# Up projection of a trunk kernel on Trainium2: in four of ten pairs, a second group of four feature blocks by seven products

## The chip, the cores and the metric

The kernel runs on one core of a Trainium2 chip. The metric is the device time of one execution in microseconds (us); a run's time is the median over several executions. The engines are named as in the profile: PE is TensorE (PEld its weight loads), DVE is VectorE, ACT is ScalarE, POOL is GpSimd, SP is SyncE, whose queue issues most weight loads.

## The reference, cut to what matters

One layer (DEPTH = 1), 256 tokens, width 2048, all in float32: a mixer, then a gated MLP, whose up projection is the subject.

```python
D_MODEL = 2048; SEQ = 256; DEPTH = 1; D_FF = 5632; CONV_FFN = 3
...
        x = x + jnp.einsum('bsd,de->bse', mixed, w_out[l])

        h = rmsnorm(x, norm_ffn_w[l])
        gate, up = jnp.split(jnp.einsum('bsd,df->bsf', h, w_up[l]), 2, axis=-1)
        gate = causal_dwconv(gate, conv_ffn_w[l]) + conv_ffn_b[l]
        x = x + jnp.einsum('bsf,fd->bsd', jax.nn.gelu(gate, approximate=False) * up, w_down[l])
    return rmsnorm(x, norm_final_w)
```

`w_up` has 2 x 5632 columns: gate and up.

## The kernel before, in words

**Precision by parts.** Every weight tile (256 rows by 512 columns, 512 KB, held as 128 x 1024) is split into a high part (`whi`, a cast on ACT) and a low part (`wlo`, raw minus high on DVE); the activations `fhl` have such parts too. A product is high x high, low x high and high x low: three matmuls of 128 x 512 for each 128 rows. The function `begin` makes the split of the next tile in the list `srcs`; `weights` hands tiles to PE and keeps two more begun. There are three buffers each of `whi` and `wlo` and four of `raw`, loaded by SP.

**Pairs.** The up projection works through 11 pairs c = 0 to 10: 512 gate columns with 512 up columns. The 256 tokens are two halves t. A plain step takes one weight tile `("plain", c, col, kp)` (col 0 gate, 1 up; kp one of eight row tiles of 256) and multiplies it with both token halves: 12 matmuls.

**Seven products.** From pair 1 on, the first four feature blocks of 128 (row tiles kp = 0 and 1, `FOUR = 0`) are done otherwise. Their four weight tiles (2 row tiles x gate and up, called quads: b11, b12, b21, b22) and the matching blocks of the activations form a 2 x 2 block product, done in seven products instead of eight: 11, T1, T2, 21, T3, 22, T4, of one weight tile and 6 matmuls each. The products named T take sums of quads, made in place on DVE by `up_sum` (line 195); sums of the activations (`ups`) are made once, by `up_sums`. The partial results meet in PSUM banks through two additions on DVE (lines 1345 and 1357) and copies on ACT.

**Order.** The list `up_steps` is written out by hand, and PE follows it. A pair's gate tiles come first, the last gate tiles alternate with the first up tiles, and the last three up tiles (`TAIL`) are set between the next pair's products T1, 11 and T2. Then follow 21, the transposes of the finished gate (`"gate"`), T3, 22, the transposes of up and T4. The elementwise work on the finished pair (convolution on ACT and DVE, line 1283, then GELU, product with up and a split, `hhi` and `hlo`) is spread over the plain steps after T4. The quads of the next pair are asked for by SP at the steps 8 to 5 ahead of its products, the sum for T1 is called 3 steps ahead. DVE, ACT and SP follow an order that a scheduler derives from the program; only PE's is fixed. Ahead of the up projection stands the output projection, in which the residual is added (`xt`), normed by feature and turned into `fhl`.

Of the kernel before, what the change touches and what calls it, by code (L numbers as in the profile page):

```python
# [8 lines left out]
F32 = mybir.dt.float32  # L9
# [5 lines left out]
P = 128  # L15
S = 256
# [19 lines left out]
def kernel(  # L36
# [58 lines left out]
    NUP = DFF // 512  # L95
    FOUR = 0
    UP_PARTS = ("T1", "11", "T2", "21", "T3", "22", "T4")
# [3 lines left out]
    for c in range(NUP):  # L101
        kps = [kp for kp in range(KD // 2) if c == 0 or kp // 2 != FOUR]
        gate_steps, up_only = ([("plain", c, col, kp) for kp in kps] for col in range(2))
        up_steps += gate_steps[:TAIL]
        for a, b in zip(gate_steps[TAIL:], up_only):
            up_steps += [a, b]
        rest = up_only[-TAIL:]
        if c + 1 == NUP:
            up_steps += rest
            break  # L110
        t1, p11, t2, p21, t3, p22, t4 = [("part", c + 1, what) for what in UP_PARTS]
        up_steps += [("loads", c + 1)]
        up_steps += [t1, rest[0], p11, rest[1], t2, rest[2], p21, ("gate", c), t3, p22, ("up", c), t4]
    for step in up_steps:
        if step[0] == "plain":
            srcs.append(up_w[step[1]][step[2]][step[3]])
        elif step[0] == "part":
            srcs.append(("up", step[1], step[2]))
    down = [cols(w_down[0], 512 * c, KF) for c in range(4)]
# [63 lines left out]
    UP_BUFFER = {"11": 0, "T1": 1, "T2": 1, "T3": 0, "21": 2, "22": 3, "T4": 1}  # L183

    def quad_load(c, n):

        i = (1, 0, 3, 2)[n]
        up_quarters[i] = fp.tile([P, 2, 512], F32, tag=f"xt{i}", name=nm("quad"))
        last_load[0] = nc.sync.dma_start(up_quarters[i], up_w[c][i % 2][2 * FOUR + i // 2]).ins

    def up_sum(what):
        b11, b12, b21, b22 = (up_quarters[i] for i in range(4))
        for out_, plus_, minus_ in {"T1": [(b12, b12, b11)], "T2": [(b12, b22, b12)],
                                    "T3": [(b11, b12, b11), (b12, b21, b12)]}[what]:
            nc.vector.tensor_tensor(out_, plus_, minus_, op=ALU.subtract)  # L195
# [14 lines left out]

    def quarter(half, chunk, what):

        if half == "up":
            return up_quarters[UP_BUFFER[what]]
# [27 lines left out]
    def begin(n):  # L242
        while len(made) < min(len(srcs), n):
            load(len(made) + 1)
            raw = loads[len(made)]
            if isinstance(raw, tuple):
                raw, plus, minus = raw
                nc.vector.tensor_tensor(raw, plus, minus, op=ALU.subtract)
            src = srcs[len(made)]
            following = {"T1": "T2", "T2": "T3"}.get(src[2]) if isinstance(src, tuple) and src[0] == "up" else None  # L250
# [4 lines left out]
            nc.scalar.copy(hi, raw)  # L255
            if shape[1] == 8:
                lo = None
                nc.vector.tensor_tensor(hi[:, :, 32:64], raw[:, :, 0:32], hi[:, :, 0:32].bitcast(F32),
                                        op=ALU.subtract)
            else:  # L260
                lo = wpool.tile(shape, F32R, tag="wlo", name=nm("wlo")) if keep is None else \
                    mtile(4 + keep, shape, F32R, nm("klo"))
                last_split[0] = nc.vector.tensor_tensor(lo, raw, hi.bitcast(F32), op=ALU.subtract).ins  # L263
                splits.append(last_split[0])
            made.append((hi, lo))
            if following is not None:
                up_sum(following)
            if isinstance(src, tuple) and src[0] != "up" and src[2] in ("T1", "T3", "T2", "T4"):
                next_quarter()
# [990 lines left out]

    def up_sums():

        h = fp.tile([P, 4, S], F32, tag="y", name=nm("whole"))
        for j in range(2):
            part = fhl[2 * FOUR + j]
            nc.vector.tensor_tensor(h[:, 2 * j : 2 * j + 2], part[:, :, 0, :].bitcast(F32),
                                    part[:, :, 1, :].bitcast(F32), op=ALU.add)
        b = fp.tile([P, 2, 4, S], F32R, tag="ups", name="ups")
        return four_sums(*by_halves(h), b[:, 0], b[:, 1])

# [20 lines left out]
    def up_part(c, pts):  # L1291
# [8 lines left out]
        else:  # L1300
            hh = fp.tile([P, 4, S], F32R, name=f"hhi{c}")
            hl = fp.tile([P, 4, S], F32R, name=f"hlo{c}")
        nc.scalar.copy(hh, y)
# [24 lines left out]

    def up_product(c, what):

        bank = banks_of.setdefault(c, {})
        if what in ("11", "21", "T4"):
            j, t = {"11": (0, 0), "21": (1, 0), "T4": (1, 1)}[what]
            high, low = (lambda kk, f=f: f(4 * FOUR + 2 * j + kk, t) for f in (fh, fl))
        else:
            n = {"T1": 0, "T2": 1, "T3": 2, "22": 3}[what]
            high, low = (lambda kk, s=s: s[:, n, kk * P : (kk + 1) * P] for s in up_ups[0])
        w = weights()
        if what == "T1":
            bank["own"] = pm()[:, 0]  # L1340
# [5 lines left out]
        ps = {"T1": "own", "21": (0, 0), "22": (1, 0)}.get(what, (0, 1))  # L1346
        high_first([(bank[ps], high, low)], w, what in ("T1", "11"))
        if what == "T1":
            own = cpool.tile([P, 512], F32, tag="sqj", name=nm("own"))
# [44 lines left out]
    for i, step in enumerate(up_steps):  # L1394
        if step[0] == "part":
            up_product(*step[1:])
            if step[2] == "T4":
                def elementwise(c=step[1] - 1, gates=gates, ups=ups):
# [9 lines left out]
        elif step[0] == "plain":  # L1408
            up_plain(*step[1:])
            if step[1:] == (0, 0, 1):  # L1410
                turned_rows()
            if step[1] == 0 and step[2:] == (0, TAIL):
                up_ups.append(up_sums())
            if step[1] == NUP - 1 and step[2] == 0:
# [204 lines left out]
```

## Time and profile before

| | |
|---|---|
| median of three runs | 1553.76 us (1552.94 to 1554.03) |
| the profiled execution, its span | 1553.06 us, 1551.3 us |
| TensorE's mean granted clock | 0.998 |
| busy: PE, PEld, DVE, ACT | 1537.5, 1268.2, 1195.4, 829.8 us |
| output projection, up projection | to about 819 us, 819 to 1307 us |
| one pair of the up projection | about 44.1 us |
| read from HBM | 301.75 MB |

Busy times are sums over the span, in which stages with different limits lie; a stage is read from its own stretch. Times in the views are us from the start of the span. A row of a timeline names its start, its duration, engine, line and operation, then in brackets the idle time ahead of it and what ended that. A load's "us to landing" runs from its issue to its last byte. A row of stretches gives, after the stretch and its length, each engine's busy time and count of instructions, then the granted clock, the mean busy share of the 16 DMA engines and GB/s.

### The profile page before, as it was taken

How to read it: one execution, taken by the hardware profiler on the slowest of the kernel's cores; microseconds unless marked ns; L12 is line 12 of the kernel's file. 1: busy time of each engine (PE TensorE's matmuls, PEld its weight loads, DVE VectorE, ACT ScalarE, POOL GpSimd, SP SyncE). 2: the span in 40 equal slices, each digit the busy share in tenths (PEclk: the TensorE clock that was granted, in tenths of full speed). 3: DMA queues.
4: the chain of work that ended last, by engine and by line, in shares of the span. 5: the costliest groups of instructions: out<-in, count | busy, mean ns of one | idle time of the engine just before them, and what ended most of it. 6: DMA issues, size and time to landing. Idle time of an engine off the chain costs nothing.

```text
span 1551.3 us, 20145 instructions
## 1 busy us (share of the span) xinstructions
PE 1537.5 (99%) x7350; PEld 1268.2 (82%) x7350; DVE 1195.4 (77%) x1713; ACT 829.8 (53%) x1038; POOL 65.1 (4%) x82
## 2 busy tenths in 40 slices
PE   9999999999999999999999999999999999999998
PEld 8888888788878888888887888888888888788886
DVE  6789858996689858887664877778778776878885
ACT  6455446454545445454454666656656665545552
POOL 1010002000100000000000000000000000000100
PEclk9999999999999999999999999999999999999999
DMA  8777757776577656675676666656666667556652
GB/s 273 212 223 211 199 153 226 213 207 182 166 231 211 197 170 200 215 209 181 215 260 205 189 190 182 186 180 199 203 200 190 188 187 267 189 190 204 221 189 92
DMA packets 167697, 310.46 MB, mean 200 GB/s; under 512 B 19458, under 2 KB 23330, under 8 KB 167470
## 3 DMA queue, kind: packets, MB, share of 16 engines
q1 hardware_dynamic: 159456, 287.37, 61.0%
q0 software_dynamic: 4032, 14.68, 2.9%
q10 hardware_dynamic: 4110, 7.13, 1.4%
q8 instruction: 57, 0.93, 0.2%
q14 instruction: 42, 0.34, 0.1%
HBM read 301.75 MB, written 7.38 MB: 199 GB/s over the span
## 4 chain that ended last, share of the span: by engine, by line
PE 96%; DMA 1%; DVE 1%; issue 1%; ACT 0%; POOL 0%; POOLq 0%; DVEq 0%; ACTq 0%
PE psg L1326 29%; PE psm L298 15%; PE psm L300 15%; PE psm L299 15%; PE psm L1311 7%; PE psg L1311 6%; PE psm L444 1%; PE psm L1383 1%; PE psg L343 1%; PE psm L1326 1%; PE psg L834 1%; DVE wlo L263 0%; DMA raw<-in_w_down_dram 0%; PE psg L836 0%; DMA vrow<-ev 0%
## 5 line engine op out<-in xcount | busy, mean ns | idle before, releaser
L255 ACT CAST whi<-raw 128x1024 fp32r<-128x1024 f32 x460 | 484.1, 1053 | 474.5 <-PE psm L299 277.0
L263 DVE TENSOR_TENSOR wlo<-raw,whi 128x1024 fp32r<-128x1024 f32 x458 | 557.1, 1220 | 169.0 <-ACT whi L255 163.2
L263 DVE TENSOR_TENSOR wlo<-quad,whi 128x1024 fp32r<-128x1024 f32 x112 | 137.1, 1224 | 73.2 <-ACT whi L255 71.9
L255 ACT CAST whi<-quad 128x1024 fp32r<-128x1024 f32 x112 | 118.1, 1055 | 107.5 <-PE psg L1326 55.9
L300 PE MATMUL psm<-wlo,xhl 128*128 128x512 f32 x432 | 169.5, 393 | 1.8 <-DVE wlo L263 1.8
L298 PE MATMUL psm<-whi,xhl 128*128 128x512 f32 x432 | 169.0, 391 | 0.0
L299 PE MATMUL psm<-whi,xhl 128*128 128x512 f32 x432 | 168.6, 390 | 0.0
L1326 PE MATMUL psg<-whi,fhl 128*128 128x512 f32 x504 | 127.9, 391 | 0.0
L1326 PEld LDWEIGHTS psg<-whi,fhl 128*128 128x128 f32 x504 | 93.9, 188 | 18.9
L300 PEld LDWEIGHTS psm<-wlo,xhl 128*128 128x128 f32 x432 | 81.1, 188 | 19.2 <-DVE wlo L263 2.6
L298 PEld LDWEIGHTS psm<-whi,xhl 128*128 128x128 f32 x432 | 81.1, 188 | 16.7
L299 PEld LDWEIGHTS psm<-whi,xhl 128*128 128x128 f32 x432 | 81.1, 188 | 16.7
L1326 PE MATMUL psg<-wlo,fhl 128*128 128x512 f32 x252 | 69.9, 389 | 0.0
L1311 PE MATMUL psm<-wlo,hhi 128*128 128x512 f32 (+1 forms) x150 | 58.1, 387 | 0.5 <-DVE wlo L263 0.5
L1311 PE MATMUL psm<-whi,hhi 128*128 128x512 f32 (+1 forms) x150 | 58.2, 388 | 0.2 <-ACT whi L255 0.2
L1311 PE MATMUL psm<-whi,hlo 128*128 128x512 f32 (+1 forms) x150 | 58.0, 386 | 0.0
L1326 PEld LDWEIGHTS psg<-wlo,fhl 128*128 128x128 f32 x252 | 47.3, 188 | 10.0
L195 DVE TENSOR_TENSOR quad<-quad,quad 128x1024 f32<-128x1024 f32 x40 | 49.0, 1225 | 7.5 <-DMA quad<-in_w_up_dram 6.5
L298 PE MATMUL psm<-whi,mhi 128*128 128x512 f32 x128 | 50.9, 397 | 0.0
L1311 PE MATMUL psg<-whi,hhi 128*128 128x512 f32 (+1 forms) x130 | 50.3, 387 | 0.1
L300 PE MATMUL psm<-wlo,mhi 128*128 128x512 f32 x128 | 50.0, 391 | 0.0
L1311 PE MATMUL psg<-whi,hlo 128*128 128x512 f32 (+1 forms) x130 | 50.0, 386 | 0.0
(428 smaller groups left out, 2939.8 us busy)
## 6 DMA issues: line engine op xcount, KB each, us to landing
raw<-in_w_in_dram SPq DMA_DIRECT2D x224, 512.0 KB, 4.3
raw<-in_w_up_dram SPq DMA_DIRECT2D x136, 512.0 KB, 4.6
raw<-in_w_down_dram SPq DMA_DIRECT2D x64, 512.0 KB, 4.7
quad<-in_w_up_dram SPq DMA_DIRECT2D x40, 512.0 KB, 4.5
raw<-in_w_out_dram SPq DMA_DIRECT2D x32, 512.0 KB, 4.0
quad<-in_w_down_dram POOLq DMA_DIRECT2D x24, 512.0 KB, 5.3
mv<-vrow SPq DMA_DIRECT2D x12, 512.0 KB, 4.5
taps<-in_conv_qkv_w_dram SPq DMA_DIRECT2D x16, 256.0 KB, 6.5
```

The costliest lines, as they stand in the source:

```text
L195: nc.vector.tensor_tensor(out_, plus_, minus_, op=ALU.subtract)
L255: nc.scalar.copy(hi, raw)
L263: last_split[0] = nc.vector.tensor_tensor(lo, raw, hi.bitcast(F32), op=ALU.subtract).ins
L298: mm(ps[:, t, :], lh(k, t), hi[:, kk, :], start=(k == 0), stop=False)
L299: mm(ps[:, t, :], ll(k, t), hi[:, kk, :], start=False, stop=False)
L300: mm(ps[:, t, :], lh(k, t), lo[:, kk, :], start=False, stop=(k == nk - 1))
L343: nc.tensor.transpose(pt[:, ff, t * P : (t + 1) * P], src[:, t, f * P : (f + 1) * P], ident)
L444: mm(ps_k0[:, t, :], part(k, t), w[:, kk, :], start=(k == 0 and w is hi and part is xh), stop=(k == KD - 1 and w is lo))
L834: mm(pg0, kq[:, h, 0, 0:P], kq[:, h, :, :], start=True, stop=True)
L1311: mm(ps[:, cs], lhs(kk), part_[:, kk, cs], start=(first and kk == 0 and n == 0), stop=(last and kk == 1 and n == 2), skip_group_check=shared)
L1326: mm(ps, lhs(kk), w[n][:, kk], start=(first and n == 0 and kk == 0 and lhs is high), stop=False, skip_group_check=True)
L1383: nc.tensor.transpose(out_[f // 2][:, f % 2, t * P : (t + 1) * P], e[:, t, f * P : (f + 1) * P], ident)
```

## The change

In pairs 1, 3, 5 and 7 (`TWO`) the feature blocks 4 to 7 (row tiles kp = 2 and 3, group `ch` = 1) are also done by seven products, ahead of group 0 in each place. The seven results of both groups are accumulated in the same banks: group 1 begins them, group 0 ends them. The pair ahead does all its gate tiles first and keeps its last six up tiles (`tail` = 6) for the places between the first six products (T1, 11 of group 1, T1, 11 of group 0, T2 of each). Then come 21, 21, the gate's transposes, T3, T3, 22, 22, up's transposes, T4, T4. The second group's quads live in the buffers of the later `hhi8`, `hlo8`, `hhi9`, `hlo9`, and are asked for in the program 12 to 9 steps ahead of the products, the first group's 6 to 3 steps ahead. The sums of T3 and T4 are now two separate calls, and sums stand behind chosen splits (`sums_behind`).

```diff
-    FOUR = 0
+    TWO = (1, 3, 5, 7)
+    chunks_of = [()] + [(1, 0) if c in TWO else (0,) for c in range(1, NUP)]
...
-        kps = [kp for kp in range(KD // 2) if c == 0 or kp // 2 != FOUR]
+        kps = [kp for kp in range(KD // 2) if kp // 2 not in chunks_of[c]]
...
+        tail = 6 if c + 1 in TWO else TAIL
...
+        parts = [[("part", c + 1, what, ch) for what in UP_PARTS] for ch in chunks_of[c + 1]]
         up_steps += [("loads", c + 1)]
-        up_steps += [t1, rest[0], p11, rest[1], t2, rest[2], p21, ("gate", c), t3, p22, ("up", c), t4]
+        if c + 1 in TWO:
+            first_four = [parts[ch][n] for ch in range(2) for n in (0, 1)] + [parts[ch][2] for ch in range(2)]
+            for a, b in zip(first_four, rest):
+                up_steps += [a, b]
+            p21, t3, p22, t4 = ([parts[ch][n] for ch in range(2)] for n in range(3, 7))
+            up_steps += p21 + [("gate", c)] + t3 + p22 + [("up", c)] + t4
+        else:
+            t1, p11, t2, p21, t3, p22, t4 = parts[0]
+            up_steps += [t1, rest[0], p11, rest[1], t2, rest[2], p21, ("gate", c), t3, p22, ("up", c), t4]
...
+            if src[1] not in TWO:
+                behind = {"T1": [(n, "T2", 0)], "T2": [(n, "T3", 0), (n, "T4", 0)]}.get(what, [])
+            else:
+                behind = {("11", 1): [(n, "T1", 0), (n + 1, "T2", 1)], ("T1", 0): [(n + 1, "T2", 0)],
+                          ("T2", 1): [(n, "T3", 1), (n + 1, "T4", 1)],
+                          ("T2", 0): [(n, "T3", 0), (n + 1, "T4", 0)]}.get((what, ch), [])
...
+    UP_HOMES = (("xt0", "xt1", "xt2", "xt3"), ("hhi8", "hlo8", "hhi9", "hlo9"))
...
-    def up_sums():
+    def up_sums(ch):
...
-    def up_product(c, what):
+    def up_product(c, what, ch):
...
+        begins, ends_ = (ch == chunks_of[c][n] for n in (0, -1))
...
-        for n in range(4):
-            if i + 8 - n < len(up_steps) and up_steps[i + 8 - n][0] == "loads":
-                quad_load(up_steps[i + 8 - n][1], n)
-        if i + 3 < len(up_steps) and up_steps[i + 3][0] == "loads":
-            up_sum("T1")
+        for n, step in enumerate(up_steps):
+            if step[0] == "loads":
+                when = (6, 5, 4, 3, 12, 11, 10, 9) if step[1] in TWO else (8, 7, 6, 5)
+                for q in sorted(range(len(when)), key=lambda q: -when[q]):
+                    if max(n - when[q], 0) == i:
+                        quad_load(step[1], q)
+                if n - 3 == i:
+                    up_sum("T1", chunks_of[step[1]][0])
```

The scheduler places DVE, ACT and SP anew. First, DVE at the beginning of a pair's products; `quad` is a tile of group 0 or 1, `raw` a plain up tile. Before, in pair 2:

```order
L263 TENSOR_TENSOR wlo_1346_7828<-quad_1326_7721,whi_1345_7826 128x1024
L195 TENSOR_TENSOR quad_1326_7721<-quad_1334_7767,quad_1326_7721 128x1024
L263 TENSOR_TENSOR wlo_1350_7850<-raw_1348_7846,whi_1349_7848 128x1024
L263 TENSOR_TENSOR wlo_1352_7866<-quad_1330_7747,whi_1351_7864 128x1024
L195 TENSOR_TENSOR quad_1330_7747<-quad_1326_7721,quad_1330_7747 128x1024
L263 TENSOR_TENSOR wlo_1357_7881<-raw_1355_7877,whi_1356_7879 128x1024
L263 TENSOR_TENSOR wlo_1359_7897<-quad_1326_7721,whi_1358_7895 128x1024
```

and now, in pair 3:

```order
L286 TENSOR_TENSOR wlo_1416_8156<-quad_1383_7991,whi_1415_8154 128x1024
L1331 TENSOR_TENSOR hlo1_8128<-y_1401_8071,hhi1_8127 128x1024
L219 TENSOR_TENSOR quad_1383_7991<-quad_1389_8016,quad_1383_7991 128x1024
L286 TENSOR_TENSOR wlo_1419_8174<-raw_1417_8170,whi_1418_8172 128x1024
L286 TENSOR_TENSOR wlo_1422_8193<-quad_1385_8002,whi_1421_8191 128x1024
L219 TENSOR_TENSOR quad_1385_8002<-quad_1383_7991,quad_1385_8002 128x1024
L286 TENSOR_TENSOR wlo_1426_8207<-raw_1424_8203,whi_1425_8205 128x1024
```

The same alternation of split, sum, split goes on; it now runs over six products in place of three, and the `hlo` of the elementwise work falls between the first split and its sum.

Second, DVE behind the last products. Before, behind pair 2's T4 (its split is the first row):

```order
L263 TENSOR_TENSOR wlo_1375_7980<-quad_1326_7721,whi_1374_7978 128x1024
L1357 TENSOR_TENSOR psg_1376_7988<-psg_1360_7901,own_1354_7875 128x512
L1283 SCALAR_TENSOR_TENSOR y_1387_8041<-psm_1373_7969,cfw_390,y_1387_8041 128x255
L263 TENSOR_TENSOR wlo_1379_7994<-raw_1377_7990,whi_1378_7992 128x1024
L1283 SCALAR_TENSOR_TENSOR y_1387_8041<-psm_1373_7969,cfw_390,y_1387_8041 128x254
L263 TENSOR_TENSOR wlo_1383_8015<-raw_1381_8011,whi_1382_8013 128x1024
L195 TENSOR_TENSOR quad_1391_8073<-quad_1391_8073,quad_1395_8099 128x1024
L1283 SCALAR_TENSOR_TENSOR y_1387_8041<-psm_1373_7969,cfw_390,y_1387_8041 128x255
```

and now behind pair 1's last T3, 22 being split (the splits of the two T4 are the rows from quads):

```order
L1389 TENSOR_TENSOR psg_1329_7710<-psg_1293_7512,own_1299_7548 128x512
L1310 SCALAR_TENSOR_TENSOR y_1347_7789<-psm_1324_7681,cfw_390,y_1347_7789 128x255
L286 TENSOR_TENSOR wlo_1331_7714<-quad_1241_7255,whi_1330_7712 128x1024
L1310 SCALAR_TENSOR_TENSOR y_1347_7789<-psm_1324_7681,cfw_390,y_1347_7789 128x254
L286 TENSOR_TENSOR wlo_1333_7724<-quad_1260_7363,whi_1332_7722 128x1024
L286 TENSOR_TENSOR wlo_1338_7747<-raw_1336_7743,whi_1337_7745 128x1024
L1310 SCALAR_TENSOR_TENSOR y_1347_7789<-psm_1324_7681,cfw_390,y_1347_7789 128x255
L219 TENSOR_TENSOR quad_1383_7991<-quad_1383_7991,quad_1385_8002 128x1024
L286 TENSOR_TENSOR wlo_1342_7761<-raw_1340_7757,whi_1341_7759 128x1024
L1310 SCALAR_TENSOR_TENSOR y_1347_7789<-psm_1324_7681,cfw_390,y_1347_7789 128x254
L286 TENSOR_TENSOR wlo_1346_7775<-raw_1344_7771,whi_1345_7773 128x1024
L219 TENSOR_TENSOR quad_1335_7741<-quad_1335_7741,quad_1339_7755 128x1024
```

The sum in the eighth row now is the T1 sum of pair 3's group 1 (its split stands in the list for pair 3 above), drawn ahead of the split of the second plain gate tile of pair 1; the T1 sum of pair 2 is the last row. It writes into the buffer that pair 1's first T4 was split from.

Third, SP in the output projection. Before:

```order
L179 DMA raw_1168_6847<-in_w_out_dram 128x2x512
L179 DMA raw_1171_6865<-in_w_out_dram 128x2x512
L179 DMA raw_1179_6908<-in_w_out_dram 128x2x512
L179 DMA raw_1182_6926<-in_w_out_dram 128x2x512
L179 DMA raw_1185_6944<-in_w_out_dram 128x2x512
L179 DMA raw_1188_6962<-in_w_out_dram 128x2x512
```

and now:

```order
L201 DMA raw_1168_6847<-in_w_out_dram 128x2x512
L213 DMA quad_1241_7255<-in_w_up_dram 128x2x512
L201 DMA raw_1171_6865<-in_w_out_dram 128x2x512
L213 DMA quad_1242_7257<-in_w_up_dram 128x2x512
L213 DMA quad_1243_7259<-in_w_up_dram 128x2x512
L213 DMA quad_1248_7296<-in_w_up_dram 128x2x512
L201 DMA raw_1179_6908<-in_w_out_dram 128x2x512
```

All four quads of pair 1's group 1 are asked for among the output projection's tiles, the last three of them ahead of raw 6908. At the same place DVE stood so before:

```order
L263 TENSOR_TENSOR wlo_1170_6851<-raw_1168_6847,whi_1169_6849 128x1024
L263 TENSOR_TENSOR wlo_1173_6869<-raw_1171_6865,whi_1172_6867 128x1024
L1199 TENSOR_TENSOR xt1_6772<-xt1_6772,psm_1130_6596 128x1024
L263 TENSOR_TENSOR wlo_1181_6912<-raw_1179_6908,whi_1180_6910 128x1024
L1218 SCALAR_TENSOR_TENSOR fhl0_6780<-psg_1166_6829,vec_381,fhl0_6780 128x256
```

and now:

```order
L286 TENSOR_TENSOR wlo_1170_6851<-raw_1168_6847,whi_1169_6849 128x1024
L219 TENSOR_TENSOR quad_1241_7255<-quad_1241_7255,quad_1242_7257 128x1024
L286 TENSOR_TENSOR wlo_1173_6869<-raw_1171_6865,whi_1172_6867 128x1024
L1222 TENSOR_TENSOR xt1_6772<-xt1_6772,psm_1130_6596 128x1024
L1241 SCALAR_TENSOR_TENSOR fhl0_6780<-psg_1166_6829,vec_381,fhl0_6780 128x256
L1241 SCALAR_TENSOR_TENSOR fhl0_6780<-psg_1167_6838,vec_381,fhl0_6780 128x256
L1241 SCALAR_TENSOR_TENSOR fhl0_6780<-psg_1166_6829,vec_381,fhl0_6780 128x256
L1289 TENSOR_TENSOR whole_1255_7334<-fhl0_6780 128x512
L1241 SCALAR_TENSOR_TENSOR fhl0_6780<-psg_1167_6838,vec_381,fhl0_6780 128x256
L1262 TENSOR_TENSOR sums_1256_7338<-whole_1255_7334 128x256
```

The T1 sum of pair 1's group 1 stands ahead of the split of raw 6865; feature scalings (`fhl`) and the first group's operand sums (`whole`, `sums`) have come ahead of the split of raw 6908, which followed the second residual addition (`xt1`).

More of the change, by code (lines that the diff above doesn't have):

```diff
@@ L265, in begin @@
             made.append((hi, lo))
-            if following is not None:
-                up_sum(following)
+            for what, ch in sums_behind.get(len(made) - 1, ()):
+                up_sum(what, ch)
             if isinstance(src, tuple) and src[0] != "up" and src[2] in ("T1", "T3", "T2", "T4"):
@@ L1346, in up_product @@
         ps = {"T1": "own", "21": (0, 0), "22": (1, 0)}.get(what, (0, 1))
-        high_first([(bank[ps], high, low)], w, what in ("T1", "11"))
-        if what == "T1":
+        high_first([(bank[ps], high, low)], w, what in ("T1", "11") and begins)
+        if not ends_:
+            pass
+        elif what == "T1":
             own = cpool.tile([P, 512], F32, tag="sqj", name=nm("own"))
```

60 lines of the change are left out of this document (35 added, 25 removed).

## The prediction

> **What bounds the kernel now.** I read the page first: its busy times, then its chain of work that ended last.
>
> ```profile
> span 1551.3 us, 20145 instructions
> PE 1537.5 (99%) x7350; PEld 1268.2 (82%) x7350; DVE 1195.4 (77%) x1713; ACT 829.8 (53%) x1038; POOL 65.1 (4%) x82
> PE 96%; DMA 1%; DVE 1%; issue 1%; ACT 0%; POOL 0%; POOLq 0%; DVEq 0%; ACTq 0%
> ```
>
> TensorE carries 96% of the chain. That is an average, so the up projection is read by itself: the stretches of one pair, and the chain inside it.
>
> ```profile
> core 0: us, PE busy (x) PEld busy (x) DVE busy (x) ACT busy (x) POOL busy (x), PEclk, DMA share, GB/s
> 961.06:1005.20 44.14, 44.14 (x203) 36.62 (x204) 34.51 (x37) 27.19 (x31) 0.00 (x0) 1.00 0.63 191
> ```
> ```profile
> 964.82 25.89 PE psg L1326 x114
> 990.71 1.36 PE psm L1326 x6
> 1004.31 0.87 PE psm L1383 x8
> ```
>
> One pair takes 44.14 us and TensorE is busy for all of it, at full clock; the chain never leaves TensorE. So a matmul less is time less, as long as the others keep up: 114 matmuls in 25.89 us are 0.2271 us each. VectorE has 44.14 - 34.51 = 9.6 us to spare in a pair, ScalarE 17, the DMA engines a third. VectorE is the one to watch, so its groups inside this pair come next (busy, mean, idle before and its cause):
>
> ```profile
> L263 DVE TENSOR_TENSOR wlo<-raw,whi 128x1024 fp32r<-128x1024 f32 x12 | 14.6, 1220 | 2.9 <-ACT whi L255 2.9
> L263 DVE TENSOR_TENSOR wlo<-quad,whi 128x1024 fp32r<-128x1024 f32 x8 | 9.8, 1225 | 5.7 <-ACT whi L255 5.5
> L195 DVE TENSOR_TENSOR quad<-quad,quad 128x1024 f32<-128x1024 f32 x4 | 4.9, 1226 | 0.6 <-DMA quad<-in_w_up_dram 0.5
> L1283 DVE SCALAR_TENSOR_TENSOR y<-psm,cfw,y 128x255 f32<-128x255 f32 (+1 forms) x8 | 3.8, 478 | 0.1
> L1357 DVE TENSOR_TENSOR psg<-psg,own 128x512 f32<-128x512 f32 x1 | 0.7, 699 | 0.4 <-PE psg L1326 0.4
> ```
>
> Its idle time is nearly all waiting for ScalarE's high halves, and those wait for TensorE to give weight buffers back: VectorE is paced by TensorE, not the reverse. VectorE's timeline gives its true pitch, shorter than the durations because neighbours overlap:
>
> ```profile
> 946.80 1.23 DVE L263 TENSOR_TENSOR wlo<-quad,whi 128x1024 fp32r<-128x1024 f32 x1 [1.49 <-ACT whi L255]
> 948.06 1.23 DVE L195 TENSOR_TENSOR quad<-quad,quad 128x1024 f32<-128x1024 f32 x1
> 949.20 1.22 DVE L263 TENSOR_TENSOR wlo<-raw,whi 128x1024 fp32r<-128x1024 f32 x1
> 950.88 1.23 DVE L263 TENSOR_TENSOR wlo<-quad,whi 128x1024 fp32r<-128x1024 f32 x1 [0.46 <-ACT whi L255]
> ```
>
> From 948.06 to 949.20 a pitch is 1.14 us; from 946.80 to 948.06 it is 1.26 us, the sum waiting for the split of the tile that it overwrites.
>
> **The change part by part.** *Fewer matmuls.* In pairs 1, 3, 5 and 7 a second group goes from four plain tiles of 12 matmuls (48) to seven products of 6 (42). 4 x 6 = 24 matmuls go: 24 x 0.2271 = 5.45 us, all on the path. Bytes from HBM stay the same: four quads take the place of four raw tiles.
>
> The weight loads' row asks for a smaller price:
>
> ```profile
> L1326 PEld LDWEIGHTS psg<-whi,fhl 128*128 128x128 f32 x504 | 93.9, 188 | 18.9
> ```
>
> If loads of 0.188 us, not the 0.2271 us pitch, were what a matmul costs here, 24 would give 4.5 us; but 25.89/114 is a start-to-start pitch over an unbroken stretch, and it is what I take. (The Trainium skill, "Perfetto Trace Analysis", section "Identifying the Most-Contended Engine", says that matmul busy time misleads and that LDWEIGHTS busy share should be read instead: 82% here. By that measure TensorE is not full, and the sum below would lose 0.9 us; the unbroken chain in the pair does not agree with it.)
>
> *More VectorE and ScalarE work in those pairs.* Three more splits (22 for 19) and four more sums: 3 x 1.14 + 4 x 1.26 = 8.5 us on VectorE, so 34.51 + 8.5 = 43.0 us, beside 44.14 - 1.36 = 42.8 us of TensorE. Taken alone such a pair fills VectorE. But the next pair is an old one: 43.0 + 34.5 = 77.5 of 86.9 us for two. What matters is where the work lies. In the first part of the products every product is followed by an up tile: VectorE does split, sum, split in 1.26 + 1.14 + 1.14 = 3.54 us while TensorE needs 18 x 0.2271 = 4.09 us. That is today's own pattern (the 0.46 us of idle above), six times for three. Then eight products stand without up tiles: 48 x 0.2271 + 2 x 0.87 = 12.6 us of TensorE, against 8 x 1.14 and two bank sums of 0.70, 10.5 us of VectorE. Then come five plain tiles, 13.6 us, with the gate's elementwise work (8 x 0.48) and two sums. I count from the end of the last T3 product on TensorE: up to the low half of the second plain gate tile VectorE must do a bank sum, three steps of the convolution, four splits and the hoisted T1 sum, about 0.7 + 1.3 + 4.6 + 1.2 = 7.8 us, and TensorE reaches that half after 22, 22, the transposes, T4, T4, one plain tile and two thirds of the next: 4 x 1.36 + 0.87 + 2.72 + 1.82 = 10.9 us. Cost on the path: 0, with some 3 us in hand, and the cover is the three-deep weight buffers. ScalarE gets 3 casts of 1.05 us more in a pair where it has 17 idle: 0. The second group's operand sums are made once, in the shapes of the first group's:
>
> ```profile
> L1266 DVE TENSOR_TENSOR whole<-fhl 128x512 f32<-128x512 f32 x2 | 1.3, 684 | 0.0
> L1242 DVE TENSOR_TENSOR ups<-sums,ups 128x1024 fp32r<-128x1024 f32 x1 | 1.2, 1220 | 0.0
> L1239 DVE TENSOR_TENSOR sums<-whole 128x256 f32<-128x256 f32 x1 | 0.4, 419 | 0.0
> ```
>
> That is 1.3 + 1.2 + 4 x 0.42 = 4.2 us of VectorE, needed only at the first pair's products, and it lies in the output projection, where the rows below leave VectorE 0.5 to 1.9 us free in 5: 0 by itself, though it lengthens the queue there.
>
> *The hoisted sum.* After an odd pair the T1 sum of the next but one pair stands in VectorE's queue ahead of plain splits, and it needs quads whose homes are only freed by T4's split. Now:
>
> ```profile
> 960.95 1.22 DVE L263 TENSOR_TENSOR wlo<-quad,whi 128x1024 fp32r<-128x1024 f32 x1
> 966.89 1.23 DVE L195 TENSOR_TENSOR quad<-quad,quad 128x1024 f32<-128x1024 f32 x1 [0.54 <-DMA quad<-in_w_up_dram]
> ```
> ```profile
> DMA to landing us min/median/max: 4.3/4.5/6.6
> ```
>
> Today the quad lands 966.89 - 962.17 = 4.7 us after T4's split. In the new order two convolution steps, two splits, 3.1 us, lie between, so VectorE stands for about 1.6 us, out of the 3 us in hand: 0. All behind it on VectorE waits with it, the low halves of the next plain tiles above all, and TensorE for them. Eight quads also go out in a row on SP's queue there, one to each of the eight products, so about one in 1.6 us. With a landing of 6.6 us the stand is 3.5 us and TensorE loses 0.4 us; with the 7.4 us that loads take where the DMA engines are full (rows below) it loses 1.2 us, at each of three places: bounds 0 to 3.6 us. I take 0, since the median is what one quad at a time shows.
>
> *Four quads pulled into the output projection.* SP asks for the second group's first four quads among the output projection's tiles, ahead of raw 6908. That stretch is full already:
>
> ```profile
> 765.00:770.00 5.00, 5.00 (x24) 4.14 (x23) 4.43 (x4) 2.26 (x3) 0.00 (x0) 1.00 0.99 334
> 770.00:775.00 5.00, 5.00 (x28) 4.23 (x27) 3.09 (x4) 3.58 (x9) 0.00 (x0) 1.00 1.05 399
> 775.00:780.00 5.00, 5.00 (x28) 4.24 (x27) 4.54 (x9) 3.88 (x10) 0.00 (x0) 1.00 0.99 328
> 780.00:785.00 5.00, 5.00 (x24) 4.14 (x23) 3.78 (x9) 3.10 (x5) 0.00 (x0) 1.00 0.97 299
> 785.00:790.00 5.00, 5.00 (x24) 4.00 (x23) 4.05 (x5) 3.06 (x3) 0.00 (x0) 1.00 0.49 175
> ```
> ```profile
> raw<-in_w_out_dram SPq DMA_DIRECT2D x10, 512.0 KB, 7.4
> xt<-in_x_dram ACTq DMA_DIRECT2D x4, 512.0 KB, 8.1
> ```
> ```profile
> 773.31 1.05 ACT L255 CAST whi<-raw 128x1024 fp32r<-128x1024 f32 x1 [1.43 <-DMA raw<-in_w_out_dram]
> 782.84 1.05 ACT L255 CAST whi<-raw 128x1024 fp32r<-128x1024 f32 x1 [0.80 <-PE psm L299]
> ```
>
> The DMA engines are saturated for 20 us, loads need 7.4 us, and raw 6908's cast already waited for its data until 773.31. Four quads are 2.10 MB: 5.3 us at 399 GB/s, 7.0 at 299. The slack: the cast at 782.84 takes the buffer that raw 6908's tile leaves (three casts later), so TensorE was on that tile for the 12 x 0.2271 = 2.7 us before it, from about 780.1, and needs its low half near 780.5. Back by the split and the cast, 1.22 + 1.05, and two hand-overs: the cast may begin at 778.1, 4.8 us later than now. So data late by 5.3 to 7.0 us stalls TensorE by 0.5 to 2.2 us. The T1 sum of pair 1 also stands earlier in VectorE's queue there, waiting for the second of these quads, and the cast of raw 6908 now stands behind two squares and four feature scalings on ScalarE, and its split behind the operand sums on VectorE. Bounds: 0, if the quads land in turns that spare raw 6908, to 7.0, if no slack is left. I take 1.5 us, within 0.5 to 2.2.
>
> *The sum.* The profiled execution took 1553.06 us (span 1551.3 and 1.76 around it). 1553.06 - 5.45 + 0 + 1.5 = 1549.1. The median of the three runs, 1553.76, is 0.7 above that execution, so 1549.8 us is my forecast, 0.25% faster. About 0.2%, 3.1 us, is what a measurement of this kernel can tell from no change.
>
> **The rivals.**
> *The burst eats the gain (no change).* The four quads delay several raw tiles in a row and the 5.3 us of transfer all turn up as TensorE waiting: 1553.76 - 5.45 + 5.3 = 1553.6; with the hoisted sums' 3.6 and the 1.5 instead, 1553.4. For it: the saturated rows and the 1.43 us wait. Against it: 4.8 us of slack, and the DMA engines fall to 0.49 busy at once after 785. Chance 0.20.
> *Weight loads price the matmul.* 24 x 0.188 = 4.5 us: 1553.76 - 4.5 + 1.5 = 1550.8, within no change. For it, the 82% of weight loads; against it, the measured pitch. Chance 0.03. (It is what the Trainium skill's rule above would lead to.)
> *VectorE becomes the bound (slower).* Place: pairs 1, 3, 5, 7. VectorE has 43.0 us of work in them; if it can't borrow from the next pair and keeps the waits that one pair shows, 0.4 for the bank sum, 0.5 for DMA and one 1.49 us wait for a cast, it needs 45.4 us where the pair now takes 44.14: 4 x 1.3 = 5.2 us, 1559.0. It decides against the change from 1.1 us of idle in such a pair. For it: 43.0 against 42.8, and strict order on its queue. Against it: most of its idle is TensorE's pace handed back, and would vanish where VectorE is late; and the next pair has 9.6 us free. Chance 0.20.
> The forecast itself, stalls under 2.3 us in all, has 0.57.
>
> **How the numbers follow.** Faster by over 0.2% means under 1550.65: 0.57. Within 0.2%: 0.20 + 0.03 = 0.23. Slower by over 0.2%, above 1556.9: 0.20. Low end: no stall at all is 1553.76 - 5.45 = 1548.3, less 0.7 for the scatter, 1547.6. High end: 1557.0 holds the rival of no change with its bounds and the lighter part of the slower one; some 0.15 lie above, 0.03 below.
>
> **What would show it.** Right: 186 - 6 matmuls in an odd pair and about 42.8 us for it, the old pairs still 44.1, TensorE's waits in the up projection as small as now; VectorE at about 43 us busy in an odd pair; in the output projection, casts that wait for DMA longer than 1.43 us, and TensorE's first waits there, 0.5 to 2.2 us. Wrong: odd pairs of 44 us or more with TensorE waiting for low halves (VectorE is the bound), TensorE waiting right after T4 behind a sum that waits for DMA (the hoisted sum), or over 3 us of waiting near 780 us (the burst).

## The result, and the profile after

The changed kernel took 1549.6 us (median of 6 runs, 1548.04 to 1551.22) beside 1554.2 for the kernel before (6 runs, 1552.94 to 1556.92): a ratio of 0.9967, 95% interval 0.9954 to 0.998. That is 0.33% faster, and 1549.8 was forecast. The profiled execution took 1548.64 us.

The page of the profile after: span, busy times, chain.

```profile
span 1546.8 us, 20166 instructions
PE 1533.0 (99%) x7326; PEld 1264.2 (82%) x7326; DVE 1227.4 (79%) x1748; ACT 842.9 (54%) x1051; POOL 65.6 (4%) x82
PE 96%; DMA 2%; issue 1%; DVE 1%; ACT 0%; POOL 0%; POOLq 0%; SPq 0%; DVEq 0%
```

TensorE has its 24 matmuls less (7326 for 7350) and only 4.5 us less busy time. To see where the span's 4.5 us come from, I cut it at three places that both kernels have: the gated rows' last transposes (L343, now L366), the first up matmul, the first down-projection matmul.

| stretch | before, us | after, us | difference |
|---|---|---|---|
| start to the last transposes | 759.76 | 758.18 | -1.58 |
| output projection | 59.44 | 61.15 | +1.71 |
| up projection | 488.64 | 483.64 | -5.00 |
| down projection to the end | 243.46 | 243.83 | +0.37 |

The first row is no effect of the change: up to there every kernel shown here runs the same instructions, and their traces give 758.18 to 760.16. The last lies in the traces' scatter too (243.04 to 244.39). So the change is +1.7 and -5.0, together 3.3 us, where the interval of the ratio is 3.1 to 7.1 us. First the up projection, in windows of two pairs (an odd and an even one, between two sets of up transposes), before and after; the last row is an old pair of the kernel after.

```profile
919.66:1007.91 88.25, 88.25 (x405) 73.20 (x404) 68.97 (x73) 54.38 (x63) 0.00 (x0) 1.00 0.63 191
```
```profile
919.89:1006.56 86.67, 86.67 (x400) 72.07 (x399) 76.00 (x80) 57.10 (x66) 0.00 (x0) 1.00 0.64 195
1224.00:1268.08 44.08, 44.08 (x203) 36.60 (x202) 34.54 (x37) 27.23 (x32) 3.09 (x4) 1.00 0.63 189
```

An odd pair takes 86.67 - 44.08 = 42.6 us, with TensorE busy throughout, and VectorE 76.00 - 34.5 = 41.5. Four times 1.5 us would be 6; the stage shows 5.0. The missing microsecond is lost ahead of pair 1: there TensorE waits for the last features, in both kernels, and in this trace its granted clock (the column after the POOL count) falls behind the wait.

```profile
827.85 0.66 PE L1235 MATMUL psm<-ident,xt 128*128 128x128 f32 x4 [2.47 <-DVE fhl L1241]
828.27 3.46 PE L1353 MATMUL psg<-whi,fhl1a 128*128 128x512 f32 x8
```
```profile
828.00:829.00 1.00, 1.00 (x7) 0.86 (x7) 0.00 (x0) 0.45 (x1) 0.00 (x0) 0.81 0.88 287
829.00:830.00 1.00, 1.00 (x4) 0.81 (x3) 0.48 (x1) 0.45 (x2) 0.00 (x0) 0.50 0.96 248
```

Eight matmuls that take 2.08 us at the same place before take 3.46, at a clock of 0.50. The trace of before has the same wait and no fall:

```profile
827.72 0.66 PE L1212 MATMUL psm<-ident,xt 128*128 128x128 f32 x4 [2.47 <-DVE fhl L1218]
828.13 2.08 PE L1326 MATMUL psg<-whi,fhl1a 128*128 128x512 f32 x8
```

In the output projection TensorE's waits (total, times, longest) and the chain of work at that place:

```profile
PE psm L321 <- ACT whi L278: 0.5, 1, 0.5
PE psm L323 <- DVE wlo L286: 0.5, 1, 0.5
```
```profile
759.29 6.81 DMA quad<-in_w_up_dram
766.12 0.37 SPq L213
766.59 11.56 DMA raw<-in_w_out_dram
778.18 1.06 ACT whi L278
779.26 1.24 DVE wlo L286
780.54 0.50 PE psm L323
```

The chain leaves TensorE and runs through a quad's load, SP's queue, a raw tile that needs 11.6 us to land, its cast and its split. That is the burst, at the place that was named. The view counts a wait from the modelled end of the matmul ahead of it; from start to start the two places lose 1.4 us, and the first matmuls behind them the other 0.3.

### The profile page after: what moved, and what is told of

Its sections match the earlier page's. It is cut to its first block, busy times and chain, and to the rows that moved or that the text cites. A ratio compares the mean times of both kernels' runs of the same rounds, so it can differ in the third digit from the quotient of the medians.

```text
span 1546.8 us, 20166 instructions
## 1 busy us (share of the span) xinstructions
PE 1533.0 (99%) x7326; PEld 1264.2 (82%) x7326; DVE 1227.4 (79%) x1748; ACT 842.9 (54%) x1051; POOL 65.6 (4%) x82
## 4 chain that ended last, share of the span: by engine, by line
PE 96%; DMA 2%; issue 1%; DVE 1%; ACT 0%; POOL 0%; POOLq 0%; SPq 0%; DVEq 0%
PE psg L1353 29%; PE psm L323 15%; PE psm L321 14%; PE psm L322 14%; PE psm L1338 7%; PE psg L1338 7%; PE psm L467 1%; PE psm L1353 1%; PE psm L1415 1%; PE psg L366 1%; PE psg L857 1%; DMA raw<-in_w_out_dram 1%; DMA quad<-in_w_up_dram 0%; PE psg L859 0%; DVE wlo L286 0%
## 5 line engine op out<-in xcount | busy, mean ns | idle before, releaser
L278 ACT CAST whi<-raw 128x1024 fp32r<-128x1024 f32 x444 | 467.8, 1055 | 440.1 <-PE psm L322 270.9
L286 DVE TENSOR_TENSOR wlo<-raw,whi 128x1024 fp32r<-128x1024 f32 x442 | 538.4, 1222 | 145.8 <-ACT whi L278 138.0
L286 DVE TENSOR_TENSOR wlo<-quad,whi 128x1024 fp32r<-128x1024 f32 x140 | 171.2, 1224 | 59.7 <-ACT whi L278 58.0
L278 ACT CAST whi<-quad 128x1024 fp32r<-128x1024 f32 x140 | 147.8, 1056 | 120.5 <-PE psg L1353 67.8
L219 DVE TENSOR_TENSOR quad<-quad,quad 128x1024 f32<-128x1024 f32 x56 | 68.5, 1223 | 11.0 <-DMA quad<-in_w_up_dram 6.0
```

## The experiments

A ratio is always to the kernel before, from runs on the same chip. Stretches are cut as in the table.

**Once more, as the yardstick.** The changed kernel unchanged.

> The changed kernel once more, on the chip and beside the runs of the kernel before that the next three share, so that differences of 1 to 3 us can be read against it. Expected: a ratio of 0.9967 to the kernel before, as measured first (0.9954 to 0.998). What its trace tells apart: the second wait of TensorE after the first up tiles, 2.5 us, was followed by 3.4 us at half clock in two of six traces (the changed kernel and the burst kernel) and not in four; if the clock falls there by chance, this trace is 1.6 us longer or not in the up projection at that place alone.

Ratio 0.9968 (0.9957 to 0.998). Output projection 61.66 us, up projection 482.58, no fall of the clock: 6.06 us off the up projection, 1.06 more than in the first trace. The wait is the same 2.47 us; why the clock falls behind it in one trace and not in another is in the last section.

**The burst: quads held back, and the burst alone.**

```diff
+        if (c, ch) == (1, 1):
+            nc.vector.tensor_copy(up_quarters[ch, i][:, 0, 0:1], xts[3][:, 0, 0:1])
         last_load[0] = nc.sync.dma_start(up_quarters[ch, i], ...)
```

> The changed kernel, with the second group's first four quads held back: each quad of pair 1 first gets one column copied from the last row block of the output projection, so that its load cannot be asked for before that block is summed; four tiny copies on VectorE (about 0.1 us each) are added, and nothing else moves. Theory: the 1.7 us that the output projection became longer (from its first transposes to the first up matmul 59.44 us before, 61.15 after) is the four quads' 2.1 MB ahead of its weight tiles. Then the stretch is 59.4 to 59.8 us again, the two waits of TensorE near 779 us are gone, and the whole is 1.3 to 1.7 us below the changed kernel: a ratio of 0.9956 to 0.9958 to the kernel before, where the changed kernel has 0.9967. Rival: the second group's operand sums and the longer queues on VectorE and ScalarE cost it, not the loads. Then the stretch stays at 61.1 us and the ratio at 0.9967. A second rival: the loads cost as much wherever they are put, and TensorE now waits 1 us or more for tiles between 822 and 850 us; the stretch shrinks, the total does not.

Ratio 0.9962 (0.9951 to 0.9974). The output projection takes 59.37 us, as before the change, and TensorE's only wait there and in the up projection is the old one:

```profile
PE psm L1237 <- DVE fhl L1243: 2.5, 1, 2.5
```

The first theory holds for the stretch: 1.8 to 2.3 us less than in the two traces of the changed kernel, with the operand sums still made in that stretch. The ratio moved by 0.0005 only, and its interval overlaps that of the changed kernel, so the gain in the whole is not resolved by this run.

The counter-test puts the four loads, and nothing else of the change, into the kernel before:

```diff
+        if i == 0:
+            for j, home in enumerate(("hhi8", "hlo8", "hhi9", "hlo9")):
+                spare = fp.tile([P, 2, 512], F32, tag=home, name=nm("spare"))
+                nc.sync.dma_start(spare, up_w[1][j % 2][2 + j // 2])
```

> The kernel before, with no second group; only the four loads of pair 1's second-group quads are added, into buffers that nobody reads, at the place on the DMA queue where the changed kernel has them (ahead of the same raw tile of the output projection). Matmuls, VectorE and ScalarE do the same work as before. Theory: the burst alone makes the output projection 1.0 to 1.7 us longer (59.44 us before), with TensorE's two waits near 779 us, so the ratio to the kernel before is 1.0006 to 1.0011. Rival 1: the place is paid for by the operand sums and queues on VectorE and ScalarE: 0 to 0.3 us, ratio 1.0000 to 1.0002. Rival 2: the burst eats what its bytes need, 5.3 us: ratio 1.0034.

Ratio 1.002 (1.0011 to 1.0028): 3.1 us slower. The output projection is 61.78 us long, 2.34 more, with the same two waits and a third:

```profile
PE psm L298 <- ACT whi L255: 0.8, 1, 0.8
PE psm L300 <- DVE wlo L263: 0.7, 2, 0.5
```
```profile
780.32 1.04 ACT L255 CAST whi<-raw 128x1024 fp32r<-128x1024 f32 x1 [1.30 <-DMA raw<-in_w_out_dram]
```

So the loads alone make all of that cost, and more than I expected of them. The up projection was 1.2 us longer in this trace, for the clock fell to 0.50 behind the 2.5 us wait here too.

**How much room VectorE has.** First without lighter neighbours:

```diff
-    TWO = (1, 3, 5, 7)
+    TWO = (1, 2, 3, 4, 5, 6, 7, 8)
```

(The quads are asked for at 4, 4, 3, 3 and 6, 6, 5, 5 steps ahead. The list of steps changes too: a changed pair has only four plain up tiles, so the last two of the next pair's first six products stand without one.)

> The changed kernel with two groups in pairs 1 to 8 instead of 1, 3, 5 and 7, the quads of a pair asked for 6 to 3 steps ahead: no old pair stands between two changed ones, so VectorE cannot borrow time from a lighter neighbour. 24 more matmuls go. Theory A (an odd pair keeps TensorE's pace by itself, VectorE's 43 us being within reach of it): every one of the eight pairs takes 42.6 us, four times 1.5 us less than the changed kernel, a ratio of 0.992 to 0.993. Theory B (VectorE at 43.0 us of work is itself the pace once it cannot borrow): 43.0 us for a pair, 1.1 us gained in each of eight, ratio 0.994 to 0.996, and TensorE shows short waits for low halves in the pairs. Rival (the slower one of the prediction: VectorE keeps its waits for casts, bank sums and quads): 45.4 us for a pair, 1.3 us more than an old one, eight times: ratio about 1.006, and TensorE waits 2 to 3 us in each pair.

Ratio 1.0016 (1.0006 to 1.0027): 24 further matmuls less, and slower than before. One pair:

```profile
1055.16:1099.74 44.58, 42.90 (x197) 35.37 (x196) 41.41 (x44) 30.20 (x35) 0.00 (x0) 1.00 0.60 189
```
```profile
DVE quad L219 <- issue: 1.8, 1, 1.8
DVE wlo L286 <- ACT whi L278: 1.1, 2, 0.7
```
```profile
PE psm L1353 <- DVE y L1310: 7.8, 5, 1.9
PE psm L1353 <- ACT e L1403: 3.1, 2, 1.7
```

VectorE works 41.4 us and stands for 3: 44.6 us a pair, near the 45.4 of the prediction's slower rival. TensorE does not wait for low halves, as that rival has it, but for the PSUM bank of the gate's transposes, which the T1 product needs and the convolution on VectorE (L1310) frees (by the view, in five of the seven waits). That VectorE's total work sets this pace is not shown: in this list four plain tiles lie between T4 and the next T1, and behind a changed pair of the changed kernel five, so T1 also asks for the bank one tile (2.7 us) earlier.

Then by adding work. In the next kernel the low halves of two gate tiles of every odd pair are written twice.

```diff
+                if len(made) in twice:
+                    last_split[0] = nc.vector.tensor_tensor(lo, raw, hi.bitcast(F32), op=ALU.subtract).ins
```

> The changed kernel; in pairs 1, 3, 5 and 7 the low half of two plain gate tiles is computed twice, which adds 2 x 1.14 = 2.3 us of VectorE to an odd pair (43.0 to 45.3 us, over the 42.6 us that TensorE needs) and nothing to TensorE. It measures how much room VectorE has left in the changed kernel. Theory (what an odd pair lacks it borrows from the next, old one, some 3 us were in hand): 0 to 0.7 us more in a pair, 0 to 3 us in all over the changed kernel, a ratio of 0.9967 to 0.9987 to the kernel before. Rival (the changed kernel already has VectorE at its limit in odd pairs): the 2.3 us are paid in full four times, 9.1 us, ratio about 1.0025, and TensorE waits for low halves in the odd pairs.

Ratio 1.0064 (1.0051 to 1.0077), worse than either. But it does not measure what it was made for: between the first and the second writing of a tile (the rows from L289 and L291) the scheduler set three instructions, the hoisted sum among them, and TensorE waits for a tile's last writer.

```profile
886.28 1.22 DVE L289 TENSOR_TENSOR wlo<-raw,whi 128x1024 fp32r<-128x1024 f32 x1
891.33 1.22 DVE L291 TENSOR_TENSOR wlo<-raw,whi 128x1024 fp32r<-128x1024 f32 x1
```
```profile
892.60 1.83 PE L1358 MATMUL psg<-wlo,fhl2a 128*128 128x512 f32 x4 [2.21 <-DVE wlo L291]
```

So work that nobody waits for, behind the hoisted T1 sum at three places:

```diff
+            if (what, ch) == ("T1", 1) and sums[0] > 0:
+                for _ in range(3):
+                    spare = fp.tile([P, 2, 512], F32, tag="s", name=nm("spare"))
+                    nc.vector.tensor_tensor(spare, out_, minus_, op=ALU.subtract)
```

> The changed kernel; after each of the three hoisted T1 sums (behind T4 of pairs 1, 3 and 5) VectorE gets three spare subtractions of 128x1024 into a buffer that nobody reads, 3 x 1.14 = 3.4 us, set among the next plain tiles' low halves. No one waits for the spare results themselves, unlike the low halves that were written twice. It asks again how much room VectorE has. Theory (1.7 to 3.3 us in hand at the next plain tiles, by the changed kernel's trace, and lighter work behind them): 0 to 0.7 us for each place, 0 to 2 us in all over the changed kernel, ratio 0.9967 to 0.998. Rival (VectorE is at its limit in odd pairs): 2.5 to 3.4 us for each place, 7.5 to 10 us, ratio 1.0015 to 1.003.

Ratio 1.0088 (1.0075 to 1.0102), 18 to 19 us over the changed kernel for 9 x 1.14 = 10.3 us of spare work: both theories are wrong. TensorE's wait, the instruction on VectorE that ended it, and the stretch behind it:

```profile
906.71 1.49 PE L1359 MATMUL psm<-whi,ups 128*128 128x512 f32 x4 [3.98 <-DVE y L1316]
```
```profile
906.09 0.47 DVE L1316 SCALAR_TENSOR_TENSOR y<-psm,cfw,y 128x254 f32<-128x254 f32 x1
```
```profile
908.00:910.00 2.00, 2.00 (x6) 1.60 (x5) 0.97 (x2) 2.00 (x3) 0.00 (x0) 0.50 0.00 0
```

It is the PSUM bank again. In the changed kernel its last convolution step and the T1 product that takes the bank are

```profile
900.16 0.48 DVE L1310 SCALAR_TENSOR_TENSOR y<-psm,cfw,y 128x254 f32<-128x254 f32 x1
```
```profile
902.50 1.07 PE L1353 MATMUL psm<-whi,ups 128*128 128x512 f32 x4
```

902.50 - 900.64 = 1.9 us in hand: by so much the step could be later without TensorE waiting. In the kernel before the same two stand at 974.1 and 990.54: 16 us. The step now ends at 906.56, 5.9 us later: 3.4 for the spare work, nearly all the rest for two low halves that the order now puts ahead of it; less 1.9 in hand, 4.0 us of waiting. Each of the three waits of 4.0 to 4.2 us is followed by 3 to 7 us at half clock, another 1.9 to 3.2 us: from the up transposes among an odd pair's products to those among the next, even pair's it is 40.5, 40.6 and 42.0 us, where the changed kernel has 34.6.

Three runs test this reading: less spare work; the same behind the last convolution step; the same where an old pair has just ended.

> The kernel with the spare subtractions again, but one instead of three behind each of the three hoisted sums (1.14 us of VectorE each). In the changed kernel's trace the gate's last convolution step ends at 900.6 us and TensorE's T1 product takes that PSUM bank at 902.5: 1.9 us in hand; the tightest low half has 1.7. Theory (what decides is how late VectorE is at those two points): one spare subtraction stays inside, 0 to 0.6 us for each place, ratio 0.9967 to 0.998. Rival (VectorE's whole work decides, and the three cost 18.6 us in proportion): 6 us, ratio 1.000 to 1.001.

Ratio 0.9979 (0.9969 to 0.9989). No wait for the bank; the three distances are 0.7, 0.2 and 0.4 us longer than 34.6, and the one wait that shows is for another of VectorE's duties, the bank sum ahead of T3:

```profile
918.67 1.19 PE L1359 MATMUL psg<-whi,ups 128*128 128x512 f32 x4 [0.51 <-DVE psg L1381]
```

```diff
         nc.scalar.activation(y, y, AF.Gelu)
+        if c in (2, 4, 6):
+            for _ in range(3):
+                spare = fp.tile([P, 4, S], F32, tag="s", name=nm("spare"))
+                nc.vector.tensor_tensor(spare, y, y, op=ALU.subtract)
```

> As many spare subtractions as in the dear kernel, three at each of three places and nearly at the same time, but behind the gate's last convolution step instead of ahead of it (the gates of pairs 2, 4 and 6, behind T4 of pairs 3, 5 and 7). They read the gate after its Gelu. VectorE's work is the same 3.4 us more. Theory (the PSUM bank that T1 needs and the convolution frees is what the dear kernel ran into): no wait of TensorE for the bank, 0 to 1.5 us for each place from later low halves, ratio 0.9967 to 0.9995. Rival (any 3.4 us more in that stretch costs the same): 18 us, ratio 1.008 to 1.009.

Ratio 1.0004 (0.9994 to 1.0013), about 6 us over the changed kernel, a third of what the same work costs ahead of the convolution. (The places are one odd pair on: behind T4 of pairs 3, 5 and 7, where the kernel with spare work behind the T1 sum has 1, 3 and 5.) The wait for the bank is gone, as expected; the bank sum takes its place at 2.3, 2.1 and 0.5 us, a little dearer than I had allowed:

```profile
1005.17 1.19 PE L1357 MATMUL psg<-whi,ups 128*128 128x512 f32 x4 [2.30 <-DVE psg L1379]
```

With `c in (1, 3, 5)` in place of (2, 4, 6), which is behind T4 of the old pairs 2, 4 and 6:

> The same three spare subtractions at three places, but behind the gate of pairs 1, 3 and 5, which VectorE works on behind T4 of the old pairs 2, 4 and 6, where by the trace it has caught up and waits for casts again. Theory (an old pair has the room that an odd one borrows): 0 to 0.7 us for each place, 0 to 2 us in all, ratio 0.9967 to 0.998. Rival (two pairs together have no room left): as dear as the others, ratio 1.004 to 1.009.

Ratio 0.9968 (0.9958 to 0.9978): nothing, three distances of 34.59 us. An old pair has room for 3.4 us, and an odd one with its successor has not: place decides, not the sum of work.

**The old wait.** All eight transposes of the last feature block ahead of the casts that read them:

```diff
+            if c == 3:
+                turn(0)
+                turn(1)
             for k2 in range(2):
+                if c < 3:
+                    turn(k2)
```

> The changed kernel; the last feature block's eight transposes stand together on TensorE, ahead of the casts that read them, so the second four no longer wait for VectorE to read the first four. Nothing else moves. Theory: TensorE's 2.5 us wait at 825 to 828 us goes, and with it the 3.4 us at half clock that follow in some runs (1.6 us lost there): 2.5 us in a run without the clock's fall, 4.1 in one with it, about 3 us below the changed kernel; ratio about 0.9947 to the kernel before. Rival: a wait takes its place, since the feature halves are made as late as now: the first plain tiles wait for high and low halves instead, and the gain is under 1 us, ratio 0.996 to 0.9967.

Ratio 0.9944 (0.9932 to 0.9956). No wait of TensorE is left in the up projection; it takes 479.62 us, 2.96 less than the trace without a fall of the clock.

> The changed kernel with both edits: the second group's first quads held back until the output projection's last block is summed, and the last feature block's eight transposes together. Theory: the two are apart in time and add up, 1.7 us (the burst) and about 3 us (the wait and the clock): the output projection 59.4 us, no wait in the first pair, ratio about 0.9936 to 0.994 to the kernel before. Rival: with the wait gone TensorE reaches the first tiles 2.5 us earlier, while the quads now load among those tiles, and waits for data there: the ratio stays at 0.995 or above, with waits for low halves between 822 and 860 us.

Ratio 0.9936 (0.9925 to 0.9948), 1544.66 us beside 1554.21, the fastest kernel of this study: output projection 59.42 us, up projection 479.45, with the transposes in one piece and the first plain tile straight behind. The median is 0.5 us below the run before it and the intervals overlap, so what holding the quads back is worth in the whole stays unresolved here too; the output projection is 1.8 us shorter than in that run's trace. The transposes:

```profile
823.32 1.04 PE L1239 MATMUL psm<-ident,xt 128*128 128x128 f32 x8
824.11 2.07 PE L1365 MATMUL psg<-whi,fhl1a 128*128 128x512 f32 x8
```

## Why the prediction was right

- *24 matmuls, 5.45 us.* Undisturbed it is 6.06 (482.58 for 488.64). The rate was right; what I left out is a bank sum. Before, the T3 product follows the gate's transposes after 0.90 us, since the bank sum ends only then; in an odd pair the sum is done ahead of them, and it follows after 0.80:

```profile
960.02 1.04 PE L1383 MATMUL psm<-ident,e 128*128 128x128 f32 x8
960.92 1.20 PE L1326 MATMUL psg<-whi,ups 128*128 128x512 f32 x4
960.18 0.69 DVE L1345 TENSOR_TENSOR psg<-psg,own 128x512 f32<-128x512 f32 x1
1136.53 1.04 PE L1383 MATMUL psm<-ident,e 128*128 128x128 f32 x8
1137.67 1.19 PE L1326 MATMUL psg<-whi,ups 128*128 128x512 f32 x4
1136.93 0.69 DVE L1345 TENSOR_TENSOR psg<-psg,own 128x512 f32<-128x512 f32 x1
```
```profile
878.96 1.04 PE L1415 MATMUL psm<-ident,e 128*128 128x128 f32 x8
879.76 1.16 PE L1353 MATMUL psg<-whi,ups 128*128 128x512 f32 x4
877.76 0.69 DVE L1375 TENSOR_TENSOR psg<-psg,own 128x512 f32<-128x512 f32 x1
```

  In the first block the first three rows stand for pairs 1, 3 and 5, at 0.1 us each; its other three are pair 7, where the bank sum ended later still and T3 followed after 1.14 us, which is 0.3 more. Together that is the 0.6. The price by weight loads, 4.5 us, is refuted: the unbroken matmul pitch is what counted here. The Trainium skill ("Perfetto Trace Analysis", section "Identifying the Most-Contended Engine") names the busy share of the weight loads, 82% here, beside the share of peak arithmetic, as measures of how close TensorE is to its limit. It has no price for a matmul there; the 4.5 us were my own step.
- *VectorE at no cost.* Right, with wrong numbers inside. The added work was over-sized: 7 us more in two pairs (76.00 for 68.97), an odd pair 41.5 us and not 43.0. The time in hand was over-sized too: at the second plain gate tile the low half is made at 891.82 and TensorE takes it at 893.44, 1.6 us and not 3:

```profile
890.60 1.22 DVE L286 TENSOR_TENSOR wlo<-raw,whi 128x1024 fp32r<-128x1024 f32 x1
```
```profile
893.44 1.07 PE L1353 MATMUL psg<-wlo,fhl2b 128*128 128x512 f32 x4
```

  And my list of those who wait behind VectorE had low halves only; the two that stood closest were a PSUM bank (1.9 us in hand, 16 before) and the bank sum behind an old pair (none). The cover that I named, three-deep weight buffers, covers neither of them. So it was luck that the bank still had 1.9 us: I had not looked at it, and two more low halves (2.3 us) ahead of its last step would have used that up. That the next, old pair lends the time was the right reason: three spare subtractions there cost nothing, and behind a changed pair about 2 us or more. The kernel with eight changed pairs in a row agrees, but its list differs in more than that.
- *The hoisted sum at no cost.* Right: VectorE stands 1.0 us for the quad (I had 1.6), and TensorE does not wait. The view has no cause for the 1.0 us ("issue"); the trace has the last packet of a quad's load, for which VectorE's queue waits there, at 889.38.

```profile
889.46 1.23 DVE L219 TENSOR_TENSOR quad<-quad,quad 128x1024 f32<-128x1024 f32 x1 [1.01 <-issue]
```

- *The burst at 1.5 us.* Right in place, cause and size: 1.7 and 2.2 us in two traces, 2.3 by itself. Raw 6908's cast begins at 778.18, 20.0 us behind the last transposes, where 13.55 stood before: 6.4 us late, within the 5.3 to 7.0, and the slack of 4.8 us held: the rival in which all of the transfer shows did not come. The sign that I had named, casts waiting over 1.43 us for data, did not show; ScalarE had other work until 777.76 and waited 0.42.

```profile
778.18 1.05 ACT L278 CAST whi<-raw 128x1024 fp32r<-128x1024 f32 x1 [0.42 <-DMA raw<-in_w_out_dram]
```

- *The sum.* 0.6 us more gain in the up projection against a burst that is 0.2 to 0.7 dearer, and in some runs a fall of the clock: the errors cancel. The 0.2 us between 1549.8 and 1549.6 is luck besides: I forecast a drop of 3.95 us from 1553.76, and measured is one of 4.6 from 1554.2, since the median of the kernel before rose by 0.4 with three more runs.

## What to carry to other kernels

When work is added to an engine beside the bound, list everything that is handed over behind it: not the tiles it feeds alone, but the PSUM banks it frees and the sums that others start from, and take the smallest time in hand. A total that fits says little: the same 3.4 us cost nothing in one place, about 2 us in a second and about 6 in a third. New loads into buffers that have been free for long go out as soon as the queue reaches them; give them a dependency that holds them back until the DMA engines have room.

## What was unexpected of the hardware

How long TensorE may stand before its clock falls is not one number. Over thirteen traces, from the output projection to the end of the up projection, seven waits of 1.0 to 1.7 us were followed by no fall; of seventeen of 1.9 to 2.8 us, seven were followed by 3.4 us at 0.50; of three of 4.0 to 4.2 us, all three, by 3.4, 3.4 and 6.8 us. The same 2.47 us wait, at the same place, had a fall behind it in four of eleven traces, each worth 1.6 us at the place and 1.1 to 1.2 over the whole up projection.

The traces show what decides. Within each trace, all changes of the granted clock stand a whole number of 3.413 us apart, as on a fixed grid (the falls at 907.36, 999.52 and 1091.68 in the kernel with nine spare subtractions ahead of the convolution: 27 of them from one to the next). Cut along its trace's grid, the 2.47 us wait lies in one window in the first of these two traces (the kernel after) and is shared by two in the second (the changed kernel once more):

```profile
825.20:828.62 3.42, 0.95 (x8) 0.73 (x7) 2.05 (x3) 1.02 (x3) 0.13 (x1) 1.00 0.81 237
828.62:832.03 3.41, 3.41 (x10) 2.64 (x9) 0.97 (x2) 1.14 (x3) 0.00 (x0) 0.50 0.84 255
```
```profile
825.11:828.52 3.41, 1.92 (x11) 1.40 (x9) 2.67 (x5) 1.77 (x5) 0.70 (x1) 1.00 0.85 243
828.52:831.93 3.41, 2.43 (x13) 2.09 (x14) 1.17 (x3) 1.36 (x3) 0.00 (x0) 1.00 0.79 229
```

A window with 2.47 us of idle has a fall behind it, windows with 1.49 and 0.98 have none. Over all thirteen traces, from the first change on record to the last, every window with 1.93 us or more of TensorE idle was followed by a fall (23 of 23), and no window with 1.85 us or less. So what looks like chance is where the wait falls on the grid; the grid itself stands elsewhere in each execution. The Trainium skill ("TensorE: Matmul & The Clock Gate", section "Part 1: The HAM clock gate (the "warmup" mystery)") gives a free-running window of about 3.4 us and a fall after an idle window. The grid and the length of the falls agree with that, but here a window needed to be idle for little more than half: 1.93 of 3.41 us were enough.
